# Second MLP of a decoder trunk: a table load that waits for an accumulating transfer

## The chip, the cores and the metric

The kernel runs on one core of a Trainium2 chip. Its time is the device time of one launch in microseconds; the number that is compared is the median over several runs. PE is the matmul engine, DVE and ACT the two elementwise engines, POOL a fourth engine that also writes the descriptors of the transfers that it starts, and SP an engine that does nothing but start transfers. All transfers, whoever starts them, run on the core's 16 DMA engines. An engine works through its own list of instructions in order, and an instruction that waits holds everything behind it on that list.

## The reference

A trunk of two layers over 512 tokens of width 1024, in float32. Layer 0 is attention, layer 1 a gated short convolution, and each is followed by a gated MLP. The change is in the MLP of layer 1:

```python
def conv_ffn(h, norm_g, w_up, conv_w, w_down):
    xn = rms_norm(h, norm_g)
    u = causal_dwconv(xn @ w_up, conv_w)        # w_up: 1024 x 5632, width-3 causal taps
    g, val = u[..., :D_FF], u[..., D_FF:]       # D_FF = 2816
    return (jax.nn.silu(g) * val) @ w_down
```

## The kernel before

**Seven products.** `xn @ w_up` is done as a fast 2x2 block product. The 1024 rows of `w_up` are cut into halves `kh` 0 and 1, and the columns into the gate half and the value half; the tokens are cut into LEFT and RIGHT. Seven products of sums of blocks (called p1, p7, p3, p6, p2, q5 and q4) take the place of eight. The columns are handled in groups of 256 of the gate half and the same 256 of the value half, so the second MLP has 11 groups, g = 0 to 10. Each product is held to float32 accuracy by splitting both sides into a high and a low part in the matmul type and doing three matmuls of the four: 2 column tiles x 4 row tiles x 3 = 24 matmuls of 128x256 for each product, 168 for a group. `halves_to` makes the two parts of a weight tile: ACT writes the high part (`whi_p`, `whi_q`, line 1051), DVE subtracts it from the source for the low part (`wlo_p`, `wlo_q`, line 1053).

**Weight tiles of one group.** Each is 128 x 4 x 256 floats, 512 KB:

- `X` is block (0,0), for p1. Later, POOL's transfer adds block (0,1) to it in place, and it serves q5.
- `Y` comes from a table in DRAM (made earlier in the kernel, from `w_up` alone) and serves p7.
- `three` is a sum of three blocks, from a second table, and serves p6. Later POOL's transfer adds the fourth block (1,0) to it in place; from then on the code calls it `four`, and it serves q4.
- `W` is block (1,0), for p2; `Z` is block (1,1), for p3, whose product is done one group later.

`X`, `Y`, `three`, `W` and `Z` are plain loads, started by SP. The two sums in place ("accumulating transfers", `add_block`, line 1140) are started by POOL. `three`, `W` and `Z` share three buffers: `Z` keeps one, and `three` of group g+1 takes the one that `W` of group g has left, while `W` of g+1 takes the one of `three` of g.

**The schedule.** `slot(g, s)` runs for s = 0 to 6, one product in each slot, in the order p1, p7, p3 (of g-1), p6, p2, q5, q4. The slot also issues the work for products to come. In the order of the code:

- s = 0: SP loads `W` of g, and then `X` and `Y` of g+1.
- s = 1 and 2: the halves of `three` (for p6) and of `W` (for p2); then POOL adds block (1,0) to `three`, which makes it `four`.
- s = 3 and 4: the halves of `X` (for q5) and of `four` (for q4).
- s = 5: `tail` of group g-1 ends with the gated product on DVE (lines 1089 and 1090), and where a block of the down product's operand is complete, POOL starts a transfer that adds one half of the operand to the other, SBUF to SBUF (line 1098, `head_blocks` or `hs_b_blocks`; the "block add" below). Then SP loads `Z` of g, and the halves of `X` of g+1 are made.
- s = 6: `first_sums` makes the halves of `Y` of g+1, POOL adds to `X` of g+1, and SP loads `three` of g+1.

The block adds come in the groups g = 1 to 6 (256 KB each in g = 1, 2, 3 and 5, two of 128 KB in g = 4, one of 128 KB in g = 6). In the second MLP the transfers and the halves' ACT instructions are pinned to the program's order (`pin`), and so the lists of SP and POOL stand as the slots write them. The first MLP uses the same class with `name` 0.

Of the kernel before, what the change touches and what calls it, by code (L numbers as in the profile page):

```python
# [17 lines left out]
F32 = mybir.dt.float32  # L18
# [4 lines left out]
ALU = mybir.AluOpType  # L23
AX = mybir.AxisListType

P = 128
# [9 lines left out]
CHUNK = 1056  # L36
# [21 lines left out]
def trunk(  # L58
# [6 lines left out]
    nc = tc.nc  # L65
# [10 lines left out]
    pin = tc.keep_in_program_order  # L76
    act, dve, pe, pool = InOrder(nc.scalar), InOrder(nc.vector), nc.tensor, nc.gpsimd
# [3 lines left out]
    wp = ctx.enter_context(tc.tile_pool(name="wp", bufs=3))  # L81
# [8 lines left out]
    def bank(tag):  # L90
        n_ps[0] += 1
        return ps.tile([P, S], F32, tag=tag, name=f"ps{tag}{n_ps[0]}", bufs={"a": 2, "b": 4, "c": 2}[tag])
# [125 lines left out]
    def behind(later, earlier):  # L218

        tc.add_manual_dep(  # L220
            later.ins, earlier.ins.name,
            mybir.DependencyInfo(mybir.DependencyClass.NoSync, mybir.DependencyReason.DATA), reason="order",
        )
# [655 lines left out]
    t = bank("c")  # L879
# [4 lines left out]
    t = bank("c")  # L884
# [119 lines left out]
    for g in range(len(units) + 2):  # L1004
# [7 lines left out]
        if g >= 2 and units[g - 2][1] == len(UNITS) - 1:  # L1012
            p = units[g - 2][0]
# [98 lines left out]
    class Sevens:  # L1112
# [20 lines left out]
                pin(made)  # L1133

        def load_one(self, g, n, src):
            t = self.st[g][n] = wp.tile([P, CHUNK], F32, tag="raw", name=f"{n}{self.name}{g}")[:, 0:1024].rearrange("p (k c) -> p k c", c=2 * P)
            self.held(nc.sync.dma_start(t, src))

        def add_block(self, g, n, kh, half):
            tc.keep_in_program_order(nc.gpsimd.dma_start(self.st[g][n], self.block_of(g, kh, half), accum_op=ALU.add))  # L1140
# [61 lines left out]
        def slot(self, g, s):  # L1202

            on, was, soon = (i in self.groups for i in (g, g - 1, g + 1))
            if self.chores:
                self.work_off(self.rate(g, s))
            form, n, fresh = (("p1", "A", True), ("p7", "T", True), ("p3", "R", False), ("p6", "R", False), ("p2", "A", False),
                              ("q5", "R", False), ("q4", "T", False))[s]
            if s == 2:
                if was:  # L1210
                    self.product(g - 1, form, n, fresh)
            elif on:
                self.product(g, form, n, fresh)
            st, p, c = self.st, g - 1, self.st.get(g)
            if s == 0:
                if was:
                    if "p3" not in st[p]:
                        self.weights_of(p, "p3", "Z")
                    self.join(p, "yg", st[p]["T"], st[p]["Xs"])
                    if on and not self.table and g not in self.aside:  # L1220
                        behind(self.joined, self.summed)
                if on:
                    self.load_one(g, "W", self.block_of(g, 1, 0))
                if soon:
                    self.load_pair(g + 1)
            elif s == 1:
                first = not was
                if on and first and not self.ahead and "p6" not in c:
                    self.weights_of(g, "p6", self.sum_of(g))
                if on and not first and self.table:  # L1230
                    self.weights_of(g, "p6", "three")
                if on:
                    act.activation(self.bank_of(g, "R"), c["A"], AF.Copy, scale=-1.0)
                if on and not first and not self.table:
                    self.weights_of(g, "p6", self.sum_of(g))
                if on and first and self.name == 0:
                    self.weights_of(g, "p2", "W")
                if soon and not self.table:
                    self.add_block(g + 1, "Y", 1, 1)
            elif s == 2:  # L1240
                if on:
                    self.kept(g, "P7s", c["T"])
                    if "p2" not in c:
                        self.weights_of(g, "p2", "W")
                    c["four"] = c[self.sum_of(g)]
                    if self.table and soon:
                        self.add_block(g, "four", 1, 0)
                    else:
                        dve.tensor_tensor(c["four"], c["four"], c["W"], op=ALU.add)
            elif s == 3:  # L1250
                if was:
                    self.early(p, st[p]["R"])
                if on:
                    self.weights_of(g, "q5", "X")
                    if not self.table:
                        self.kept(g, "Xs", c["R"])
                        self.weights_of(g, "q4", "four")
                        self.fourth = self.rest
            elif s == 4:
                if on and self.table:  # L1260
                    self.kept(g, "Xs", c["R"])
                    self.weights_of(g, "q4", "four")
            if was and s != 2:
                self.tail(p, s)
            if s == 5:
                if on:
                    self.load_one(g, "Z", self.block_of(g, 1, 1))
                    self.open_wides(g)
                    if soon and not self.table:
                        self.weights_of(g + 1, "p1", "X")  # L1270
                        if g + 1 in self.aside:
                            self.three_of(g + 1)
                    self.left(g, c["A"])
                if soon and self.table:
                    self.weights_of(g + 1, "p1", "X")
                elif on and self.ahead and not soon:
                    self.weights_of(g, "p3", "Z")
            elif s == 6:
                if on:
                    self.join(g, "yv", c["R"], c["P7s"])  # L1280
                if soon:
                    self.first_sums(g + 1)
# [507 lines left out]
    with tc.tile_pool(name="mlp1", bufs=1, reuse_waits="tile") as mp:  # L1790
# [3 lines left out]
        raw = RawForms(up, (place(4, 4), place(8, 4)), s0, s1)  # L1794
# [48 lines left out]
        def slot(g, s):  # L1843
            up.slot(g, s)
            if g == 0 and s in more:
                more[s]()
        mlp(1, norm, mp, (blocks, [(lambda g=g, s=s: slot(g, s)) for g in range(HF + 1) for s in range(7)]))


# [24 lines left out]
```

## Time and profile before

| what | us |
|---|---|
| median of 3 runs (lowest to highest) | 1097.05 (1096.64 to 1101.11) |
| the profiled execution's own time | 1097.78 |
| span of the profiled execution, first to last instruction | 1096.0 |
| PE busy in the span | 1082.0 |
| DVE / ACT / POOL busy in the span | 959.6 / 685.8 / 183.5 |
| second MLP's sum-of-four transfers, first and last start | 765.8 / 948.2 |

The profile lists instructions by engine with their start in us from the span's start. A transfer's row shows the instruction that starts it, on SP ("SPq") or POOL; it lands some us later. In the trace `three` and `four` have one name, `three`: a row of POOL on `three<-in_ffn_w_up` is the accumulating transfer for the sum of four, a row of SP on `three<-t` the table load, and `whi_q<-three` is the first use of the finished sum of four.

### The profile page before, as it was taken

The numbers are of one execution on the slowest core, as the hardware profiler recorded it, in microseconds if no ns is written. First come the engines' busy times: TensorE is split into PE (matmuls) and PEld (weight loads), VectorE is DVE, ScalarE is ACT, GpSimd is POOL, SyncE is SP. The second block draws the span as 40 slices with busy tenths as digits, with TensorE's granted clock in tenths as the row PEclk, the third lists the DMA queues.
The fourth block names the chain that finished last, engine by engine and source line by source line (L and its number), as shares of the span: only waits on it lengthen the run. The fifth ranks groups of instructions, "written<-read, shape, count | busy, mean of one in ns | idle before, by whom it ended". The sixth has DMA issues, their size and how long they took to land.

```text
span 1096.0 us, 21688 instructions
## 1 busy us (share of the span) xinstructions
PE 1082.0 (99%) x8781; PEld 1027.7 (94%) x8781; DVE 959.6 (88%) x1483; ACT 685.8 (63%) x1021; POOL 183.5 (17%) x208
## 2 busy tenths in 40 slices
PE   9999999999999999999999999999999999999998
PEld 7888787879999999999999899999999999999998
DVE  5788898997899888899989889977899899999886
ACT  7466677655466776777557655546656556667653
POOL 4011111111011312014311001001021121014310
PEclk9999999999999999999999999999999999999999
DMA  7668878688767988899974866598879877899961
GB/s 199 163 166 220 188 182 218 163 224 220 202 152 201 223 211 208 214 270 211 232 192 109 181 173 145 137 274 195 218 185 219 184 199 189 219 268 210 239 158 59
DMA packets 178116, 214.21 MB, mean 195 GB/s; under 512 B 7676, under 2 KB 143916, under 8 KB 178016
## 3 DMA queue, kind: packets, MB, share of 16 engines
q0 software_dynamic: 53280, 95.34, 45.4%
q1 hardware_dynamic: 124576, 117.42, 33.8%
q8 instruction: 69, 1.13, 0.4%
q14 instruction: 31, 0.25, 0.1%
q10 hardware_dynamic: 160, 0.07, 0.0%
HBM read 205.72 MB, written 44.04 MB: 228 GB/s over the span
## 4 chain that ended last, share of the span: by engine, by line
PE 71%; DVE 12%; issue 9%; DMA 5%; ACT 2%; POOL 0%; SPq 0%; DVEq 0%; POOLq 0%; ACTq 0%
PE psb L1107 16%; PE psb L357 15%; PE psb L1750 9%; PE psa L1750 8%; PE psa L1107 6%; PE psa L357 4%; DMA three<-in_ffn_w_up 3%; DVE wlo_p L1053 2%; PE psb L733 2%; PE psa L830 2%; DVE wlo L334 1%; PE psc L357 1%; PE psc L805 1%; PE psb L615 1%; DMA Xc<-in_conv_w_in 1%
## 5 line engine op out<-in xcount | busy, mean ns | idle before, releaser
L1107 PE MATMUL psb<-p_hi,wlo_p 128*128 128x256 f32 x480 | 132.5, 276 | 0.9 <-DVE wlo_p L74 0.9
L1107 PE MATMUL psb<-p_hi,whi_p 128*128 128x256 f32 x480 | 132.6, 276 | 0.0
L1107 PE MATMUL psb<-p_lo,whi_p 128*128 128x256 f32 x480 | 132.5, 276 | 0.0
L333 ACT ACTIVATE whi<-raw 128x1024 fp32r<-128x1024 f32 (+2 forms) x77 | 79.0, 1027 | 65.0 <-PE psb L357 22.4
L334 DVE TENSOR_TENSOR wlo<-raw,whi 128x1024 fp32r<-128x1024 f32 (+2 forms) x77 | 90.9, 1180 | 20.2 <-ACT whi L333 20.0
L357 PE MATMUL psb<-hs_a,whi 128*128 128x512 f32 (+1 forms) x312 | 93.3, 369 | 0.0
L1107 PEld LDWEIGHTS psb<-p_hi,wlo_p 128*128 128x128 f32 x480 | 90.0, 188 | 1.2 <-DVE wlo_p L74 1.2
L1107 PE MATMUL psb<-q_hi,wlo_q 128*128 128x256 f32 x320 | 89.4, 279 | 1.1 <-DVE wlo_q L1053 1.1
L1107 PEld LDWEIGHTS psb<-p_hi,whi_p 128*128 128x128 f32 x480 | 90.1, 188 | 0.0
L1107 PEld LDWEIGHTS psb<-p_lo,whi_p 128*128 128x128 f32 x480 | 90.1, 188 | 0.0
L1107 PE MATMUL psb<-q_hi,whi_q 128*128 128x256 f32 x320 | 88.8, 277 | 1.2 <-ACT whi_q L1051 1.0
L1107 PE MATMUL psa<-p_hi,wlo_p 128*128 128x256 f32 x320 | 89.4, 279 | 0.0
L1107 PE MATMUL psa<-p_hi,whi_p 128*128 128x256 f32 x320 | 88.5, 277 | 0.0
L1107 PE MATMUL psb<-q_lo,whi_q 128*128 128x256 f32 x320 | 88.5, 277 | 0.0
L1107 PE MATMUL psa<-p_lo,whi_p 128*128 128x256 f32 x320 | 88.5, 276 | 0.0
L357 PE MATMUL psb<-hs_a,wlo 128*128 128x512 f32 (+1 forms) x208 | 69.5, 359 | 0.0
L1107 PEld LDWEIGHTS psb<-q_hi,wlo_q 128*128 128x128 f32 x320 | 60.0, 188 | 2.3 <-DVE wlo_q L1053 1.8
L357 PEld LDWEIGHTS psb<-hs_a,whi 128*128 128x128 f32 x312 | 52.4, 188 | 10.2 <-issue 3.2
L1750 PE MATMUL psb<-act,whi 128*128 128x256 f32 x352 | 61.1, 278 | 0.7 <-DVE act L1055 0.7
L1107 PEld LDWEIGHTS psb<-q_hi,whi_q 128*128 128x128 f32 x320 | 60.1, 188 | 1.8 <-ACT whi_q L1051 1.2
L1107 PEld LDWEIGHTS psa<-p_hi,wlo_p 128*128 128x128 f32 x320 | 60.0, 188 | 1.0 <-DVE wlo_p L1053 0.6
L1107 PEld LDWEIGHTS psa<-p_hi,whi_p 128*128 128x128 f32 x320 | 60.1, 188 | 0.0
(551 smaller groups left out, 3697.7 us busy)
## 6 DMA issues: line engine op xcount, KB each, us to landing
t<-in_ffn_w_up POOLq DMA_DIRECT2D x24, 768.0 KB, 8.1
raw<-in_attn_w_in SPq DMA_DIRECT2D x24, 512.0 KB, 5.8
t<-in_ffn_w_up POOLq DMA_DIRECT2D x12, 1024.0 KB, 9.8
X<-in_ffn_w_up SPq DMA_DIRECT2D x20, 512.0 KB, 5.1
Y<-t SPq DMA_DIRECT2D x20, 512.0 KB, 6.6
three<-t SPq DMA_DIRECT2D x20, 512.0 KB, 5.9
W<-in_ffn_w_up SPq DMA_DIRECT2D x20, 512.0 KB, 4.0
Z<-in_ffn_w_up SPq DMA_DIRECT2D x20, 512.0 KB, 5.0
```

What stands on the lines that cost most here:

```text
L333: return (act.activation(hi_, raw[:, at_], AF.Copy), dve.tensor_tensor(lo_, raw[:, at_], f32(hi_), op=ALU.subtract))
L334: dve.tensor_tensor(lo_, raw[:, at_], f32(hi_), op=ALU.subtract))
L357: made = [pe.matmul(acc[:, c], w[x], rhs[y][:, c], start=first and x + y + c.start == 0, stop=last and x == 1 and c.stop == S) for x, y in ...
L615: pe.matmul(acc, lhs[0], w[0], start=first, stop=False)
L733: pe.matmul(ss[e][:, c:c + wide], ql[rows, b * P:n], kl[rows, 0:wide], start=first and b == bs[0], stop=last and b == bs[-1])
L805: pe.transpose(t[:, k * P:(k + 1) * P], w[:, e, k * P:(k + 1) * P], ident)
L830: pe.matmul(out_, w, t[:, first:first + step * (NB - k - 1) + 1:step, :], start=k == 0 and i == 0, stop=k == NB - 1 and i == 1)
L1053: rest = dve.tensor_tensor(lo, src, f32(hi), op=ALU.subtract)
L1107: pe.matmul(to, w[a][:, k, c], x[b][:, k, :], start=fresh and i + k + t == 0, stop=i == 1 and k == 3 and t == 2, skip_group_check=not fresh)
L1750: pe.matmul(part, l, r[:, c], start=begin and o + t + c.start == 0, stop=end and t == 2 and o + c.start > 0, skip_group_check=not fresh)
```

## The change

In the slot s = 5 of the second MLP, right after SP's load of `Z` of g, the tile `three` of group g+1 is allocated, and POOL gets a `tensor_tensor` of one column: it writes the first element of each partition of the new `three`, and reads the first element of each partition of `four` of group g. The table load of `three` of g+1 in the slot s = 6 is unchanged but writes over that element, so SP has to wait for the POOL instruction, and the POOL instruction has to wait until the accumulating transfer into `four` of g has landed. What is computed stays the same.

```diff
         def load_one(self, g, n, src):
-            t = self.st[g][n] = wp.tile([P, CHUNK], F32, tag="raw", name=f"{n}{self.name}{g}")[:, 0:1024].rearrange("p (k c) -> p k c", c=2 * P)
-            self.held(nc.sync.dma_start(t, src))
+            if n not in self.st[g]:
+                self.place_one(g, n)
+            self.held(nc.sync.dma_start(self.st[g][n], src))
+
+        def place_one(self, g, n):
+            self.st[g][n] = wp.tile([P, CHUNK], F32, tag="raw", name=f"{n}{self.name}{g}")[:, 0:1024].rearrange("p (k c) -> p k c", c=2 * P)
+
+        def place_three(self, g):
+            self.place_one(g, "three")
+            to, other = self.st[g]["three"][:, 0, 0:1], self.st[g - 1]["four"][:, 0, 0:1]
+            pin(pool.tensor_tensor(to, other, other, op=ALU.add))
...
             if s == 5:
                 if on:
                     self.load_one(g, "Z", self.block_of(g, 1, 1))
+                    if soon and self.name == 1:
+                        self.place_three(g + 1)
                     self.open_wides(g)
```

The lists of PE, DVE, ACT and SP hold the same instructions in the same order as before; POOL's holds ten more. Where they stand on POOL's list, around the sum of four of group 1 (in these names the digit after `three` or `X` is the layer, 1, and the next ones the group; the brackets name the semaphores that an instruction waits on, DMASW those of POOL's transfers, DMAHW those of SP's). Before:

```order
L1140 DMA X11_9542<-in_ffn_w_up 128x4x256 [waits DMAHW0_49,DVE_49,Pool_49]
L1140 DMA three11_9751<-in_ffn_w_up 128x4x256 [waits DMAHW4_49,DMAHW3_49,DMAHW7_49,DMASW5_49,DVE_49]
L1098 DMA head_blocks1_9948<-head_blocks1_9948 128x2x256 [waits DVE_49,PE_49]
L1140 DMA X12_9786<-in_ffn_w_up 128x4x256 [waits DMAHW5_49,DMASW2_49,DVE_49]
L1140 DMA three12_9993<-in_ffn_w_up 128x4x256 [waits DMAHW0_49,DMAHW4_49,DMASW3_49,DVE_49]
```

The same place on POOL's list with the change:

```order
L1149 DMA X11_9542<-in_ffn_w_up 128x4x256 [waits DMAHW0_49,DVE_49,Pool_49]
L1149 DMA three11_9709<-in_ffn_w_up 128x4x256 [waits DMAHW3_49,DMASW5_49,DVE_49]
L1098 DMA head_blocks1_9949<-head_blocks1_9949 128x2x256 [waits DVE_49,PE_49]
L1146 TENSOR_TENSOR three12_9955<-three11_9709 128x1 [waits DMAHW4_49,DMASW5_49,Activation_49]
L1149 DMA X12_9787<-in_ffn_w_up 128x4x256 [waits DMAHW5_49,DMASW2_49,DVE_49]
L1149 DMA three12_9955<-in_ffn_w_up 128x4x256 [waits DMAHW0_49,DVE_49]
```

The new instruction stands behind the sum of four of group 1 and also behind the block add of `head_blocks`, and ahead of the sum into `X` of group 2; the same holds for the new instructions of the groups g = 1 to 6. In the groups without a block add (g = 0, 7, 8 and 9) it stands right behind the sum of four. SP's list at the same place, before:

```order
L1137 DMA Z11_9952<-in_ffn_w_up 128x4x256 [waits DMAHW2_49,DVE_49]
L1137 DMA three12_9993<-t160_1896 128x4x256 [waits DMAHW4_49,DMAHW0_49,DVE_49]
L1137 DMA W12_10026<-in_ffn_w_up 128x4x256 [waits DMAHW1_49,DMASW5_49,DVE_49]
L1128 DMA X13_10028<-in_ffn_w_up 128x4x256 [waits DMASW4_49]
L1129 DMA Y13_10029<-t173_1894 128x4x256 [waits DMAHW3_49]
```

And with the change:

```order
L1138 DMA Z11_9953<-in_ffn_w_up 128x4x256 [waits DMAHW2_49,DVE_49]
L1138 DMA three12_9955<-t160_1896 128x4x256 [waits DMAHW0_49,DMAHW4_49,DVE_49,Pool_49]
L1138 DMA W12_10028<-in_ffn_w_up 128x4x256 [waits DMAHW1_49,DMASW5_49,DVE_49]
L1128 DMA X13_10030<-in_ffn_w_up 128x4x256 [waits DMASW4_49]
L1129 DMA Y13_10031<-t173_1894 128x4x256 [waits DMAHW3_49]
```

The order is the same; the load of `three` has got the wait on POOL, and the loads of `W`, `X` and `Y` stand behind it.

## The prediction

> **What bounds the kernel now.** I read the page first, then the chain of waits inside the second MLP, then POOL's, SP's and ACT's instructions in order of time over one quiet group, and last the DMA engines' work in stretches cut at their pauses. From the page, and from the chain of waits (start us, us, what) at group 4 and at a place where PE runs freely:
>
> ```profile
> PE 1082.0 (99%) x8781; PEld 1027.7 (94%) x8781; DVE 959.6 (88%) x1483; ACT 685.8 (63%) x1021; POOL 183.5 (17%) x208
> ...
> 847.25 1.22 DVE wlo_p L1053
> 849.19 7.63 DMA three<-in_ffn_w_up
> 856.85 1.06 ACT whi_q L1051
> 988.61 2.73 PE psb L1107 x24
> ```
>
> PE is busy almost everywhere, and one product (24 matmuls) takes 2.73 us when nothing is missing, so a group cannot be shorter than 7 x 2.73 = 19.1 us. The chain shows the loop that runs beside it: low part of `three`, sum of four, high part of the sum, and so on. The instant at which the sum of four is first used (I call it L) is seen on ACT (start us, us, what, idle before and what ended it):
>
> ```profile
> 795.34 1.06 ACT L1051 ACTIVATE whi_q<-three 128x1024 fp32r<-128x1024 f32 x1 [0.91 <-DMA three<-in_ffn_w_up]
> 835.29 1.06 ACT L1051 ACTIVATE whi_q<-three 128x1024 fp32r<-128x1024 f32 x1 [1.61 <-DMA three<-in_ffn_w_up]
> 856.85 1.06 ACT L1051 ACTIVATE whi_q<-three 128x1024 fp32r<-128x1024 f32 x1 [3.91 <-DMA three<-in_ffn_w_up]
> 876.48 1.06 ACT L1051 ACTIVATE whi_q<-three 128x1024 fp32r<-128x1024 f32 x1 [1.85 <-DMA three<-in_ffn_w_up]
> 886.68 1.04 ACT L1051 ACTIVATE whi_p<-three 128x1024 fp32r<-128x1024 f32 x1
> 888.63 1.04 ACT L1051 ACTIVATE whi_p<-W 128x1024 fp32r<-128x1024 f32 x1
> 892.09 1.06 ACT L1051 ACTIVATE whi_q<-X 128x1024 fp32r<-128x1024 f32 x1 [0.61 <-DMA X<-in_ffn_w_up]
> 895.96 1.06 ACT L1051 ACTIVATE whi_q<-three 128x1024 fp32r<-128x1024 f32 x1 [1.10 <-DMA three<-in_ffn_w_up]
> 915.49 1.06 ACT L1051 ACTIVATE whi_q<-three 128x1024 fp32r<-128x1024 f32 x1 [1.74 <-DMA three<-in_ffn_w_up]
> ```
>
> ACT waits for the sum of four each time. From L of group 5 to L of group 6 is 895.96 - 876.48 = 19.48 us, 0.4 over the floor of 19.1: PE and this loop are nearly balanced, and a sum that lands later is paid by PE. Group 4 shows it, 856.85 - 835.29 = 21.56. From L of group 1 to L of group 7, the six groups with block adds, it is 915.49 - 795.34 = 120.15, of which 6 x 19.1 = 114.6 are PE's floor. So the most that any change of this loop can save there is 5.5 us.
>
> The DMA engines in stretches of group 5 to 6, and two of group 4 (stretch and its length, then busy time and instructions of PE, PEld, DVE, ACT, POOL, the clock, DMA share, GB/s):
>
> ```profile
> 871.70:872.50 0.80, 0.80 (x10) 0.80 (x9) 0.80 (x2) 0.80 (x2) 0.04 (x1) 1.00 0.11 31
> 872.50:875.90 3.40, 3.40 (x33) 3.40 (x32) 3.00 (x5) 2.13 (x4) 0.00 (x0) 1.00 1.13 180
> 875.90:877.20 1.30, 1.30 (x14) 1.30 (x13) 0.93 (x2) 0.72 (x1) 0.00 (x0) 1.00 0.94 331
> 877.20:879.90 2.70, 2.70 (x24) 2.54 (x24) 2.32 (x3) 2.36 (x3) 0.00 (x0) 1.00 0.01 5
> 879.90:885.20 5.30, 5.30 (x47) 5.17 (x46) 5.26 (x8) 1.06 (x1) 2.50 (x2) 1.00 0.93 270
> 885.20:891.20 6.00, 6.00 (x55) 6.00 (x54) 6.00 (x8) 5.02 (x7) 1.24 (x1) 1.00 1.13 235
> 892.00:895.30 3.30, 3.30 (x32) 3.30 (x31) 2.17 (x4) 2.77 (x4) 0.00 (x0) 1.00 1.12 179
> 851.20:856.50 5.30, 5.30 (x49) 5.30 (x49) 3.87 (x5) 1.74 (x4) 0.00 (x0) 1.00 1.00 197
> 856.50:860.20 3.70, 1.96 (x15) 1.56 (x14) 2.27 (x5) 2.95 (x3) 0.07 (x1) 1.00 0.00 0
> ```
>
> With the issue times below, the rows are read so: 872.5 to 875.9 is the sum of four (3.4 us at 180 GB/s), 875.9 to 877.2 the table load of `three` behind it (1.3 us at 331), then a pause of 2.7, then `W`, `X` and `Y` (5.3 us), then the block add, the sum into `X`, and `Z` (6.0 us). The engines work 3.4 + 1.3 + 5.3 + 6.0 = 16.0 of the 19.4 us between the ends of two sums of four (875.9 and 895.3), and rest 3.4. In group 4 the sum and the table load were mixed (5.3 us for both, not 4.7), and PE then worked 1.96 of 3.70 us, a loss of 1.74.
>
> **The change part by part.** POOL and SP over the same group:
>
> ```profile
> 870.45 1.29 POOL L1140 DMA_DIRECT2D three<-in_ffn_w_up  x1 [6.39 <-DVE wlo_p L1053]
> 880.30 1.19 POOL L1098 DMA_DIRECT2D hs_b_blocks<-hs_b_blocks  x1 [8.56 <-DVE hs_b_blocks L1090]
> 882.04 1.31 POOL L1140 DMA_DIRECT2D X<-in_ffn_w_up  x1 [0.54 <-DVE wlo_p L1053]
> ...
> 871.98 0.37 SPq L1137 DMA_DIRECT2D three<-t  x1
> 878.83 0.37 SPq L1137 DMA_DIRECT2D W<-in_ffn_w_up  x1
> 879.80 0.50 SPq L1129 DMA_DIRECT2D Y<-t  x1
> ```
>
> *Added: ten POOL instructions of one column.* The nearest rows are the kernel's other one-column holds:
>
> ```profile
> L297 POOL TENSOR_TENSOR hold<-raw x2: 927/964/1001, 557.9 to 1052.9; 128x1 f32<-128x1 f32 x2
> L1570 POOL TENSOR_TENSOR hold<-Xc x1: 326/326/326, 707.3 to 707.3; 128x1 f32<-128x1 f32 x1
> ```
>
> So each takes 0.33 to 1.0 us. POOL is 17% busy; what is behind it is the sum into `X`, held at most 0.8 us.
>
> *Moved: the table load of `three`, and with it `W`, `X` and `Y`.* By name the new wait is for the sum of four. But on POOL's list the new instruction stands behind the block add, which waits for DVE's product (8.56 us at 880.30), and that product is made after L. In the groups g = 1 to 6 SP is therefore released when POOL has finished issuing the block add, at 880.30 + 1.19 = 881.49, plus 0.33 to 1.0 for the new instruction: about 882. The load of `three` goes from 871.98 to 882, 10 us later, and `W` from 878.83 to 882.4; `X` and `Y` follow, 3 us later than now. In the groups 0, 7, 8 and 9 SP is released right after L, when the engines rest (2.7 us at 877.2), and a load of 1.3 us fits there.
>
> *What that does to the engines.* They rest from the end of the sum of four, 875.9, to the first bytes of the block add. POOL's issue of the sum of four ends at 870.45 + 1.29 = 871.74 and its bytes begin at 872.5, so 0.76 later; the block add's begin at 881.49 + 0.76 = 882.25. That is a rest of 6.35 us where it was 0.8 and 2.7. From there they have all the work of a group ahead of them, and the next sum of four is the last piece (`Z` and `Y` are issued before it). The new instruction itself is covered: SP's `W` shows first bytes at 879.9, 1.07 after its issue, so the load of `three` is ready at about 883.1, and the block add's 256 KB at 180 GB/s last until 883.7.
>
> With the same work, 16.0 us, the sum of four ends at 882.25 + 16.0 = 898.25, and the loop has 898.25 - 875.9 = 22.35 us where it had 19.4. If `W`, `X` and `Y`, now queued without gaps, each run as `three` did (1.3 us, 3.9 for the 5.3), it is 20.95. `three` ran behind another transfer as these will, so I take a value nearer to the low end, 21.4. PE cannot make it up, for it stands for the sum of four.
>
> *Group by group* (now, then): group 1: its block add was issued until 801.41 by the rows
>
> ```profile
> 800.22 1.19 POOL L1098 DMA_DIRECT2D head_blocks<-head_blocks  x1 [10.13 <-DVE head_blocks L1090]
> 860.12 0.89 POOL L1098 DMA_DIRECT2D head_blocks<-head_blocks  x1 [9.65 <-DVE head_blocks L1090]
> 861.08 0.86 POOL L1098 DMA_DIRECT2D hs_b_blocks<-hs_b_blocks  x1
> 899.25 0.89 POOL L1098 DMA_DIRECT2D hs_b_blocks<-hs_b_blocks  x1 [8.00 <-DVE hs_b_blocks L1090]
> ```
>
> 6.07 after L where group 5 has 881.49 - 876.48 = 5.01, so 21.4 + 1.06, about 22.45. Groups 2, 3 and 5: 21.4 each. Group 4: two block adds until 861.94, 5.09 after L: 21.5. Group 6: until 900.14, 4.18 after L, and half the bytes (0.7 us less): 19.85. Sum 22.45 + 3 x 21.4 + 21.5 + 19.85 = 128.0, against 120.15: **7.85 us lost**; that includes the 1.74 which group 4 gets back, since there the sum of four no longer runs mixed with the table load. The ends are 20.95 (5.15 lost) and 22.35 (13.55 lost). For the groups 7 to 9 I put a gain of 0.4 in all, nearest to group 9's (ACT waited there 2.26, against 1.74 to 1.85 in the quiet groups):
>
> ```profile
> 954.49 1.06 ACT L1051 ACTIVATE whi_q<-three 128x1024 fp32r<-128x1024 f32 x1 [2.26 <-DMA three<-in_ffn_w_up]
> ```
>
> *Is anything else late?* `three` would have its bytes by 883.7 + 1.3 = 885.0 and, with the 0.56 from last byte to use at L (876.46), be there at 885.6; its use is at 886.68. `W` at 886.9, its use 888.63. The sum into `X` would come at about 892, as now (892.09). So the sum of four is the one that is late.
>
> Net: 7.85 - 0.4 = 7.45 on the span: 1096.0 becomes 1103.4. The profiled execution took 1097.78, 1.8 over its span; the median of the runs is 1097.05, so the forecast is 1097.05 + 7.45 = **1104.5 us**, by its own terms 1101.8 to 1110.2.
>
> **The rivals.**
>
> *A: the sums and loads share the engines at a loss.* The block add and the sum into `X` now arrive among four loads. Group 4's row shows 0.6 us more for two mixed transfers; three such pairs in a group would cost up to 1.0 us more in five groups: 1109.5. The Trainium skill, "DMA: Bandwidth & Descriptors", section "Queues, rings and completion order", says that an engine takes turns between its queues packet by packet, which would mix them always. The trace shows both: the mixed stretch at 851.2, and a block add that got nothing until the loads ahead of it were through, since it landed 8.5 us after its issue:
>
> ```profile
> DMA to landing us min/median/max: 8.5/8.5/8.5
> ```
>
> By that rule the sum of four would end no earlier, since all the work is still ahead of it.
>
> *B: the wait is free.* If what is queued were done when the sum of four arrives (about 892), nothing would move: 1097. Against it: from 882.25 to 892 are 9.75 us, and the pieces take at best 6.0 + 4 x 1.3 = 11.2.
>
> *C: the other side, faster.* The table load leaves the engines to the sum of four, which lands sooner: group 4's 1.74 comes back, and the 0.4 us by which each quiet group exceeds PE's floor go in part. That is 1.7 + 6 x 0.2 = 3, about 1094. It decides if SP is released at L and not by the block add. For it speaks that the engines' rest of 2.7 us then takes the load; against it, POOL's list in the six groups.
>
> **How the numbers follow.** Forecast 0.57, A 0.13, B 0.18, C 0.12. Range 1095.5 to 1110.5: it leaves out C and half of A. A measurement of this kernel can tell about 0.5% (5.5 us) from no change, so faster means below 1091.5 and slower above 1102.5. Nearly nine tenths of the forecast and A are slower: 0.50 + 0.13 = 0.63. Faster needs all of the loop's 5.5 us: 0.03. Same is the rest, 0.34.
>
> **What would show it.** SP's load of `three` behind the block add, at about L + 5.5 in the groups 1 to 6 and right after L in 7 to 9; a DMA rest of some 6 us after each sum of four, then no pause until the next one; L to L of 21 to 22 us there, with PE idle before q4. Wrong would be: L to L still at 19.5 with the load that late (the engines were faster than their rows), `three` or `W` awaited by ACT (then p6 or p2 stalls, not q4), or a sum of four that lands while `Y` or `Z` are still under way.

## The result, and the profile after

The changed kernel takes 1111.74 us (median of 4 runs, 1110.49 to 1112.27), the kernel before 1097.24 beside it (1096.64 to 1101.11): a ratio of 1.0118, interval 1.0105 to 1.0131. The medians are 14.5 us apart; the ratio gives 13.0. The direction is the predicted one. The size is nearly twice the forecast's 7.45 us by the medians, 1.7 times by the ratio. The time lies 1.2 us above the range; by the ratio, from the forecast's own 1097.05, it would be 1110.0, just inside it.

The profiled execution took 1110.49 us with a span of 1108.7, 12.7 more than before. ACT's instructions that use the sum of four first (start us, us, what, idle before and what ended it), from group 1 to group 7:

```profile
794.12 1.06 ACT L1051 ACTIVATE whi_q<-three 128x1024 fp32r<-128x1024 f32 x1 [0.56 <-DMA three<-in_ffn_w_up]
817.75 1.06 ACT L1051 ACTIVATE whi_q<-three 128x1024 fp32r<-128x1024 f32 x1 [1.18 <-DMA three<-in_ffn_w_up]
839.46 1.06 ACT L1051 ACTIVATE whi_q<-three 128x1024 fp32r<-128x1024 f32 x1 [2.83 <-DMA three<-in_ffn_w_up]
862.45 1.06 ACT L1051 ACTIVATE whi_q<-three 128x1024 fp32r<-128x1024 f32 x1 [4.04 <-DMA three<-in_ffn_w_up]
884.51 1.06 ACT L1051 ACTIVATE whi_q<-three 128x1024 fp32r<-128x1024 f32 x1 [1.85 <-DMA three<-in_ffn_w_up]
906.65 1.06 ACT L1051 ACTIVATE whi_q<-three 128x1024 fp32r<-128x1024 f32 x1 [2.75 <-DMA three<-in_ffn_w_up]
928.31 1.06 ACT L1051 ACTIVATE whi_q<-three 128x1024 fp32r<-128x1024 f32 x1 [2.37 <-DMA three<-in_ffn_w_up]
```

From L1 to L7 it is 928.31 - 794.12 = 134.2 us where it was 120.15: 14.0 more, the whole loss. L1 itself came 1.2 us earlier than in the kernel before, and what lies behind L7 is 0.1 shorter; both lie outside the change's six groups. The six stretches are 23.6, 21.7, 23.0, 22.1, 22.1 and 21.7. All the loss is where a block add stands ahead of the new instruction, as predicted.

POOL's and then SP's instructions in group 5:

```profile
888.33 1.19 POOL L1098 DMA_DIRECT2D hs_b_blocks<-hs_b_blocks  x1 [10.98 <-DVE hs_b_blocks L1090]
889.06 0.75 POOL L1146 TENSOR_TENSOR three<-three 128x1 f32<-128x1 f32 x1
```

```profile
889.84 0.37 SPq L1138 DMA_DIRECT2D three<-t  x1
890.33 0.92 SPq L1138 DMA_DIRECT2D W<-in_ffn_w_up  x1
891.29 0.68 SPq L1128 DMA_DIRECT2D X<-in_ffn_w_up  x1
892.01 0.57 SPq L1129 DMA_DIRECT2D Y<-t  x1
```

The load of `three` starts 889.84 - 884.51 = 5.33 us after L (predicted: about 5.5), and not because of the sum of four, which landed just ahead of L: the new instruction stands behind the block add, which waited 10.98 us for DVE. `W`, `X` and `Y` follow at once. In group 7, without a block add, the new instruction runs right at L (928.31) and SP behind it:

```profile
928.41 0.19 POOL L1146 TENSOR_TENSOR three<-three 128x1 f32<-128x1 f32 x1 [6.87 <-DVE uv L466]
```

```profile
928.63 0.37 SPq L1138 DMA_DIRECT2D three<-t  x1
```

The DMA engines from group 5 to group 6, cut where their work changes (stretch and its length, busy time and instructions of PE, PEld, DVE, ACT and POOL, the clock, DMA share, GB/s):

```profile
884.20:890.10 5.90, 5.90 (x51) 5.63 (x50) 5.15 (x7) 3.59 (x4) 1.52 (x3) 1.00 0.00 0
890.10:892.20 2.10, 2.10 (x20) 2.10 (x20) 2.10 (x4) 0.54 (x1) 1.26 (x1) 1.00 1.10 155
892.20:895.30 3.10, 3.10 (x30) 3.10 (x29) 3.07 (x5) 1.34 (x2) 0.00 (x0) 1.00 0.98 291
895.30:900.00 4.70, 4.70 (x44) 4.70 (x43) 4.51 (x6) 4.08 (x5) 1.28 (x1) 1.00 1.16 244
900.00:902.60 2.60, 2.60 (x25) 2.60 (x25) 0.82 (x2) 1.46 (x2) 0.00 (x0) 1.00 1.09 373
902.60:905.80 3.20, 2.75 (x24) 2.55 (x24) 3.20 (x5) 1.30 (x3) 0.00 (x0) 1.00 1.12 194
905.80:906.70 0.90, 0.90 (x11) 0.90 (x9) 0.30 (x1) 0.05 (x1) 0.00 (x0) 1.00 0.05 7
```

The engines rest until 890.1, then work without a pause until 905.8: the block add, loads, the sum into `X` mixed with loads, loads, and last the sum of four. Behind it comes only a tail of 0.4 us on about one engine. Cut in the same way, where the work has run out on all but one or two engines, the six stretches are (us):

| group | from L to the first bytes | first bytes to the end of the work | end of the work to next L, with its tail | L to L |
|---|---|---|---|---|
| 1 | 6.7 | 15.6 | 1.35 | 23.6 |
| 2 | 5.65 | 15.6 | 0.45 | 21.7 |
| 3 | 5.65 | 15.6 | 1.75 | 23.0 |
| 4 | 4.75 | 15.9 | 1.4 | 22.1 |
| 5 | 5.6 | 15.7 | 0.85 | 22.1 |
| 6 | 4.75 | 15.9 | 1.0 | 21.7 |
| sum | 33.1 | 94.3 | 6.8 | 134.2 |
| the forecast's own terms | 34.9 | 89.6 | 3.5 | 128.0 |

The work has no pause of more than 0.3 us in it but for group 6, whose 15.9 us contain one of 0.9 (912.2 to 913.1).

### The profile page after: what moved, and what is told of

Same layout as the page of the kernel before. It is cut to its first block, busy times and chain, and to the rows that moved or that the text cites. A ratio compares the mean times of both kernels' runs of the same rounds, so it can differ in the third digit from the quotient of the medians.

```text
span 1108.7 us, 21715 instructions
## 1 busy us (share of the span) xinstructions
PE 1087.7 (98%) x8781; PEld 1031.4 (93%) x8781; DVE 960.3 (87%) x1483; ACT 685.7 (62%) x1021; POOL 187.2 (17%) x218
## 5 line engine op out<-in xcount | busy, mean ns | idle before, releaser
L334 DVE TENSOR_TENSOR wlo<-raw,whi 128x1024 fp32r<-128x1024 f32 (+2 forms) x77 | 90.8, 1179 | 21.5 <-ACT whi L333 21.3
L1107 PEld LDWEIGHTS psb<-q_lo,whi_q 128*128 128x128 f32 x320 | 61.1, 191 | 0.0
```

The source lines that it names most:

```text
L334: dve.tensor_tensor(lo_, raw[:, at_], f32(hi_), op=ALU.subtract))
L1107: pe.matmul(to, w[a][:, k, c], x[b][:, k, :], start=fresh and i + k + t == 0, stop=i == 1 and k == 3 and t == 2, skip_group_check=not fresh)
```

## The experiments

Nine kernels were run; the kernel before ran beside each set, at 1098.6 to 1098.9 us, so ratios are what is compared.

### Ahead of the block add

The block add is held back until the new instruction stands on POOL's list.

```diff
                     if soon and self.name == 1:
                         self.place_three(g + 1)
+                        self.flush()
...
-                blocks.held = not layer and p < HF - 1
+                blocks.held = bool(layer) or p < HF - 1
...
-        up.tail, up.conv = tail, conv
+        up.tail, up.conv, up.flush = tail, conv, blocks.add_up
```

> The change, but in the groups 1 to 6 the new one-column instruction stands ahead of the block add on POOL's list instead of behind it; all else is in the order of the changed kernel. My theory (the cost is the place behind the block add, which holds SP some 5.5 us past the arrival of the sum of four): SP's load of three starts within 1 us of that arrival in all ten groups, W, X and Y start as in the kernel before, the periods from one sum of four to the next are 19.2 to 19.8 us, and the time is 1094 to 1097.5 us. The rival (any delay of the table load behind the sum of four costs it, wherever the instruction stands): 1105 us or more, with periods over 20.5.

Measured: 1097.0 us, ratio 0.9981 (0.9972 to 0.9991). Its POOL and SP in group 4, and ACT's L3, L4 and L7:

```profile
854.26 0.19 POOL L1146 TENSOR_TENSOR three<-three 128x1 f32<-128x1 f32 x1 [4.68 <-DVE uv L466]
857.45 0.90 POOL L1098 DMA_DIRECT2D head_blocks<-head_blocks  x1 [3.00 <-DVE head_blocks L1090]
```

```profile
854.48 0.37 SPq L1138 DMA_DIRECT2D three<-t  x1
```

```profile
834.40 1.06 ACT L1051 ACTIVATE whi_q<-three 128x1024 fp32r<-128x1024 f32 x1 [1.93 <-DMA three<-in_ffn_w_up]
854.15 1.06 ACT L1051 ACTIVATE whi_q<-three 128x1024 fp32r<-128x1024 f32 x1 [2.10 <-DMA three<-in_ffn_w_up]
...
913.05 1.06 ACT L1051 ACTIVATE whi_q<-three 128x1024 fp32r<-128x1024 f32 x1 [1.97 <-DMA three<-in_ffn_w_up]
```

The wait for the sum of four is the same as in the change, ten times, and the loss is gone: SP starts `three` 0.33 us after L. What costs is the place behind the block add. This version also takes 0.2% less than the kernel before. L3 to L4 is 19.75 us (21.56 before), 1.8 less; the stretch L1 to L7, whose L1 is 794.44, is 118.6, 1.5 less. So in this trace the whole gain is the pair of transfers in group 4 that ran mixed before, and the other five groups together gave 0.3 back.

### Without the wait for the sum of four

```diff
-            to, other = self.st[g]["three"][:, 0, 0:1], self.st[g - 1]["four"][:, 0, 0:1]
+            to, other = self.st[g]["three"][:, 0, 0:1], ones
```

> The change, but the new instruction reads a constant instead of the finished sum of four, so that it doesn't wait for that transfer; it stands at the same place, behind the block add in the groups 1 to 6. My theory (the wait for the sum of four never decides in those groups, the list order does): SP's load of three starts as late as in the changed kernel, and the time is its own, 1109 to 1113 us. The rival (the named wait is what costs): back to 1096 to 1099 us.

Measured: 1112.64 us, ratio 1.0124 (1.0107 to 1.0141), the changed kernel's time. Its POOL in group 5:

```profile
889.62 1.19 POOL L1098 DMA_DIRECT2D hs_b_blocks<-hs_b_blocks  x1 [11.13 <-DVE hs_b_blocks L1090]
890.35 0.76 POOL L1146 TENSOR_TENSOR three<-ones 128x1 f32<-128x1 f32 x1
```

The instruction no longer reads the sum of four and runs at the same place, right behind the block add. The wait that the change is named for never decides in these groups.

### Only the groups without a block add

```diff
-                    if soon and self.name == 1:
+                    if soon and self.name == 1 and g in (0, 7, 8, 9):
```

> The new instruction only in the groups 0, 7, 8 and 9, where no block add stands ahead of it; the groups 1 to 6 are as in the kernel before. My theory: the load lands in the rest of the DMA engines there, nothing is lost, 1096.3 to 1097.6 us against 1097.2 of the kernel before. The rival (each held load costs its share of the 14.5 us, 1.45 for each of ten): 1103 us.

Measured: 1098.03 us, ratio 0.9990 (0.9981 to 1.0000). The four new instructions cost nothing. The predicted gain of 0.4 us there is smaller than what this interval can show.

### PE kept busy in group 4

In the changed kernel PE's clock drops once, in group 4. The windows of the changed kernel, clock third from the right:

```profile
862.00:866.00 4.00, 1.69 (x7) 1.48 (x8) 2.46 (x5) 2.95 (x3) 0.27 (x1) 0.75 0.00 0
866.00:870.00 4.00, 4.00 (x21) 4.00 (x20) 4.00 (x6) 0.30 (x1) 3.15 (x4) 0.50 0.65 97
870.00:874.00 4.00, 4.00 (x34) 4.00 (x34) 3.97 (x7) 2.92 (x4) 0.00 (x0) 0.90 1.04 323
```

At the clock of 0.50 only 21 matmuls start in 4 us, where group 5's row above has 44 in 4.7. It looked like a second cost of the late sum, so it was taken away:

```diff
+                if s == 6 and self.name == 1 and g == 4:
+                    spare = bank("c")
+                    for _ in range(18):
+                        pe.matmul(spare[:, 0:HT], self.st[g]["q5"][0][:, 0, 0:P], self.forms["q5"][0][:, 0, :], start=True, stop=True)
```

> The change, with 18 matmuls of q5's shape that nothing reads (18 x 0.113 = 2.0 us, work that isn't part of the computation) between q5 and q4 of group 4, where PE stood idle for 2.1 us and the granted clock then was 0.50 for some 7 us. The theory that the low clock is paid for: the clock stays at 1.0 there, and the time falls by 2.5 to 3 us against the changed kernel, to about 1108.9. The theory that the loop of transfers sets the time and the low clock lies beside it: the clock stays at 1.0 and the time is within 0.5 us of the changed kernel's, 1111.2 to 1112.2.

Measured: 1113.71 us, ratio 1.0138 (1.0122 to 1.0153), no faster than the changed kernel. The same windows here, and ACT's L4 and L5:

```profile
862.00:866.00 4.00, 3.69 (x31) 3.29 (x29) 1.00 (x2) 1.84 (x2) 0.00 (x0) 1.00 0.09 12
866.00:870.00 4.00, 3.46 (x27) 3.30 (x28) 4.00 (x8) 1.77 (x3) 2.10 (x3) 1.00 0.26 37
```

```profile
864.16 1.06 ACT L1051 ACTIVATE whi_q<-three 128x1024 fp32r<-128x1024 f32 x1 [4.10 <-DMA three<-in_ffn_w_up]
885.91 1.06 ACT L1051 ACTIVATE whi_q<-three 128x1024 fp32r<-128x1024 f32 x1 [1.85 <-DMA three<-in_ffn_w_up]
```

The clock stayed at 1.00, and L4 to L5 is 21.75 us against 22.06: 0.3, not 2.5 to 3. The low clock lies beside the loop of transfers, which sets when the next sum of four comes. (The matmuls of the two kernels' ends stand in a slightly different order, so the whole times are a rougher guide here than the stretch.)

### Two groups alone

```diff
-                    if soon and self.name == 1:
+                    if soon and self.name == 1 and g in (2, 5):
```

> The new instruction, behind the block add as in the changed kernel, only in the slots of the groups 2 and 5; the other groups are as in the kernel before. If each late load costs its own group's stretch and nothing else: two of the six losses, 2.3 to 2.6 us each, so about 1102 us against 1097.2 of the kernel before, with the loss in the periods L2 to L3 and L5 to L6 alone. If the losses of neighbouring groups feed each other (a late load of one group pushing the next one's): clearly less, 2 us or under, about 1099.

Measured: 1106.83 us, ratio 1.0066 (1.0052 to 1.0081): 7.9 us by the medians, 7.3 by the ratio, for two of the six groups. The loss is where it was expected, L2 to L3 and L5 to L6, but these are 24.75 and 23.6 us, 5.4 and 4.1 more than before instead of 2.3 to 2.6. ACT's L2 and L3, then POOL's and SP's start of the two transfers ahead of L3:

```profile
815.74 1.07 ACT L1051 ACTIVATE whi_q<-three 128x1024 fp32r<-128x1024 f32 x1 [1.00 <-DMA three<-in_ffn_w_up]
840.49 1.06 ACT L1051 ACTIVATE whi_q<-three 128x1024 fp32r<-128x1024 f32 x1 [6.00 <-DMA three<-in_ffn_w_up]
```

```profile
829.23 1.29 POOL L1149 DMA_DIRECT2D three<-in_ffn_w_up  x1 [6.63 <-DVE wlo_p L1053]
```

```profile
830.75 0.37 SPq L1138 DMA_DIRECT2D three<-t  x1
```

A held load alone is dearer, since the next one is not held: it is queued at 830.75 while the late work is still being done, and its bytes share the engines with the sum of four. From L2 the work now ends 22.8 us later (838.5) instead of the changed kernel's 21.3, and from there to L3 it takes 2.0 instead of 0.45. So neither expectation was right. In the changed kernel, as I read it, each hold also keeps the next table load away from the sum of four and so pays back part of the loss; no run takes that one load away.

### A small block add

The block add keeps 32 of its 256 columns; the rest of that sum is left out.

```diff
         def add_up(self):
+            w = 32 if self.layer else HT
             for k0, k1 in self.sums:
                 tc.keep_in_program_order(
-                    nc.gpsimd.dma_start(self.block("b", k0, k1 - k0), self.block("a", k0, k1 - k0), accum_op=ALU.add))
+                    nc.gpsimd.dma_start(self.block("b", k0, k1 - k0)[:, :, 0:w], self.block("a", k0, k1 - k0)[:, :, 0:w], accum_op=ALU.add))
```

> The change, with block adds of 32 columns instead of 256 in the second MLP (the rest of that sum is left out of the computation). POOL's list is the same, so SP is released as late as in the changed kernel; the DMA engines have 224 KB less to do in five groups and 112 KB less in group 6, which at the 180 GB/s of an accumulating transfer is 1.25 and 0.6 us. If the amount of work behind the rest sets the end of the sum of four, the stretch from L1 to L7 (134.2 us in the changed kernel) falls by 5 x 1.25 + 0.6 = 6.9 us, and the time to about 1105. If the chain of single latencies (release, first bytes, landing) sets it, or the block add runs beside the others for nothing: within 1 us of the changed kernel, 1111 to 1113.

Measured: 1108.26 us, ratio 1.0083 (1.0066 to 1.0100). ACT's L1 and L7:

```profile
794.68 1.06 ACT L1051 ACTIVATE whi_q<-three 128x1024 fp32r<-128x1024 f32 x1 [0.51 <-DMA three<-in_ffn_w_up]
...
925.63 1.06 ACT L1051 ACTIVATE whi_q<-three 128x1024 fp32r<-128x1024 f32 x1 [2.20 <-DMA three<-in_ffn_w_up]
```

The stretch L1 to L7 is 130.95 us, 3.2 less than in the changed kernel: half of the 6.9 that the amount of work would give, and more than nothing. An estimate from the traces gives a likely reason: in the changed kernel's group 5 the load of `three` is queued at 889.84, and where its bytes found the engines free they came 1.0 us after that (912.10 to 913.1 in group 6), so it could have begun at about 890.85. The block add's bytes run from 890.1 to 891.9. So some 0.75 of its 1.8 us fill time in which the engines have nothing else, and only the rest can be saved.

### Only W, X and Y late

```diff
             self.place_one(g, "three")
-            to, other = self.st[g]["three"][:, 0, 0:1], self.st[g - 1]["four"][:, 0, 0:1]
-            pin(pool.tensor_tensor(to, other, other, op=ALU.add))
+            self.place_one(g, "W")
+            pin(pool.tensor_tensor(self.st[g]["W"][:, 0, 0:1], ones, ones, op=ALU.add))
```

> The new instruction stands behind the block add as in the changed kernel, but writes into the tile of W, not into that of three: the table load of three starts as in the kernel before, and only W, and X and Y behind it on SP's list, wait for the block add (3 us later than in the kernel before instead of 10). My theory: the load of three is worked off in the DMA engines' rest again, so 1.3 us less lie ahead of the next sum of four, or up to 1.8 with what a mixed load takes; the periods of the six groups are 20.7 to 21.2, and the time is 1104 to 1107 us. The rival (only the load of three is what must not be late): 1097 to 1099 us. The other rival (W, X and Y being late is all that counts): 1111 to 1113.

Measured: 1104.35 us, ratio 1.0045 (1.0031 to 1.0060), about 5.4 us lost by the medians, 4.9 by the ratio. SP in group 3, and ACT's L1 and L7:

```profile
841.88 0.37 SPq L1138 DMA_DIRECT2D three<-t  x1
844.87 0.37 SPq L1138 DMA_DIRECT2D W<-in_ffn_w_up  x1
```

```profile
796.83 1.06 ACT L1051 ACTIVATE whi_q<-three 128x1024 fp32r<-128x1024 f32 x1 [0.48 <-DMA three<-in_ffn_w_up]
...
922.52 1.06 ACT L1051 ACTIVATE whi_q<-three 128x1024 fp32r<-128x1024 f32 x1 [1.47 <-DMA three<-in_ffn_w_up]
```

The stretch is 125.7 us, 20.95 a group in the mean (20.15 to 22.56), as my theory had it. The lateness of `W`, `X` and `Y` alone costs 125.7 - 120.15 = 5.5 us; with that of `three` on top, which then isn't loaded in the engines' rest any more, it is 134.2, another 8.5. The loss grows with the work that is pushed out of the rest.

### The loads ahead of the block add

The version with the new instruction ahead of the block add, but in the groups 1 to 6 the new instruction reads one column of DVE's finished product (`newest`) instead of the sum of four.

```diff
+            if 1 <= g - 1 <= 6:
+                other = self.newest(2 * (g - 2) + 1)
```

> In the groups 1 to 6 the new instruction waits for DVE's product (it reads the product's tile) and stands right ahead of the block add, so SP is released 0.6 to 0.9 us earlier than in the changed kernel, and the block add starts 0.6 to 0.75 us later; all else is as in the changed kernel. In the changed kernel's trace the DMA engines run the block add alone for 1.8 us before the loads' first bytes come, and group 6, with half a block add, has 0.9 us of it and then a pause. If the start of the loads sets the end of the sum of four: each of the six stretches is 0.6 to 0.9 us shorter, L1 to L7 falls from 134.2 to 129 to 131, and the time to about 1108 us. If the block add's start sets it, as my prediction counted: 0.6 to 0.75 us longer each, about 1116. If only the amount of work counts: within 1 us of 1112.

Measured: 1110.49 us, ratio 1.0101 (1.0084 to 1.0118). The profiled execution was the longest of its four (1115.14); its L1 and L7 are 134.3 us apart, as in the changed kernel. ACT's L3 and L4, and the engines between them (the first load bytes come at 849.7):

```profile
844.79 1.06 ACT L1051 ACTIVATE whi_q<-three 128x1024 fp32r<-128x1024 f32 x1 [2.87 <-DMA three<-in_ffn_w_up]
867.07 1.06 ACT L1051 ACTIVATE whi_q<-three 128x1024 fp32r<-128x1024 f32 x1 [1.62 <-DMA three<-in_ffn_w_up]
```

```profile
849.70:854.20 4.50, 4.50 (x41) 4.39 (x40) 4.46 (x7) 1.52 (x2) 1.75 (x2) 1.00 0.93 250
854.20:861.20 7.00, 7.00 (x64) 7.00 (x63) 6.15 (x8) 4.83 (x7) 1.28 (x1) 1.00 1.15 246
861.20:865.80 4.60, 2.85 (x25) 2.65 (x24) 2.02 (x3) 2.76 (x4) 0.00 (x0) 1.00 1.09 239
```

The loads' first bytes come 4.9 us after L, against 7.6 in the changed kernel's group 3, where the block add's come at 5.65. But the block add's bytes are then done among the others, and the work takes 16.1 us, not 15.6. The theory that the block add's start sets the end (1116) falls. Between the other two the run doesn't decide. The ratio of 1.0101 lies at what 1108 us would be (1.0098) and under the changed kernel's 1.0118, though the intervals overlap; the stretch of 134.3 us, seen in the one execution with a profile, is that of the amount of work and not the 129 to 131 of the loads' start. In this trace the first five groups together are 1.6 us longer than in the changed kernel, and group 6 is 1.5 us shorter (932.61 - 912.43 = 20.2): there the loads come before the half block add, the pause of 0.9 us is gone, and the work takes 14.6 us.

### One group ahead

The version with the new instruction ahead of the block add, but with that instruction in group 4 alone.

```diff
                     if soon and self.name == 1:
-                        self.place_three(g + 1)
+                        if g == 4:
+                            self.place_three(g + 1)
+                        self.flush()
...
```

> The new instruction ahead of the block add, in the slot of group 4 alone, where the table load and the sum of four ran mixed in the kernel before (L3 to L4 was 21.56 us); all other groups as in the kernel before. If the gain of the version with the instruction ahead of every block add is this one pair of transfers: the stretch L3 to L4 falls to 19.7 us, and the time is 1.8 us under the kernel before, a little better than that version, ratio 0.9984. If the other groups gain too: less than half of that, ratio 0.9992 or more.

Measured: 1097.54 us, ratio 0.9987 (0.9977 to 0.9998), and L3 to L4 is 20.2 us in its trace (854.58 - 834.38), 1.36 less than before. That is most of the gain of the version with all groups (0.9981), with one instruction; the two intervals overlap, so a gain in other groups is neither shown nor excluded.

## Why the prediction was right in direction and wrong in size

**Right: where and how.** SP's release behind the block add, 5.3 us after L in group 5; the rest of the engines; no pause from then to the next sum of four but the one in group 6; stretches of about 22 us; nothing lost in the groups 7 to 9. PE waits ahead of q4 in four of the six stretches, most in group 4 (wait of PE for the high part of the sum of four: us in total, times, longest):

```profile
PE psb L1107 <- ACT whi_q L1051: 2.1, 1, 2.1
```

Before L2 it was p2 that stood, see below, and before L5 PE ran at half clock. The two runs that move the instruction ahead of the block add and that take its named wait away show that the place on POOL's list is the cause, they don't only agree with it.

**Wrong: the work behind the rest.** The step that failed is "`three` ran behind another transfer as these will, so I take a value nearer to the low end, 21.4". It put 15.05 us of work behind the rest; the traces show 15.6 to 15.9, just under the "same work" of 16.0 that stood beside it as the upper end. Over six groups that is 94.3 against 89.6, 4.7 of the 6.2 us that were missing. Queued loads do run faster, but only the later ones: 373 GB/s in 900.0 to 902.6, and 291 in 892.2 to 895.3. At 524 kB a load these are 1.4 and 1.8 us, not 1.3. And in group 6 the "half the bytes (0.7 us less)" saved nothing: its work took 15.9, because the loads start 1.8 us behind the block add's first bytes (913.1 and 911.35) and the half block add fills only part of that. The run with the small block add shows the same from the other side.

**Wrong: the landing.** The forecast took 0.56 us from last byte to use, from one quiet group. After the change it is 0.45 to 1.75 with the tail, 6.8 in all against 3.5. In group 3 the tail looks so:

```profile
860.70:862.10 1.40, 0.76 (x7) 0.56 (x5) 0.00 (x0) 0.00 (x0) 0.00 (x0) 1.00 0.08 12
```

A share of 0.08 is about one of the 16 engines at work for 1.4 us, while ACT waits. The Trainium skill, "DMA: Bandwidth & Descriptors", section "Why a DMA increments its semaphore by 16 and not by 1", says that the engines finish independently and that only the last of 16 reports makes the transfer complete; the row agrees. In the quiet groups of the kernel before, the next load's bytes follow the sum of four at once, so whether it had such a tail can't be seen there; why the last engine is late was not tested.

**The start** was 1.8 us better than its term (33.1 against 34.9), mostly in group 4, whose first block add had its bytes 1.1 us sooner. It hid that much of the other two misses.

**"Nothing else is late"** was wrong. `W` was awaited in one group, `three` in another, and the sum into `X` in five:

```profile
810.73 1.06 ACT L1051 ACTIVATE whi_p<-W 128x1024 fp32r<-128x1024 f32 x1 [3.09 <-DMA W<-in_ffn_w_up]
...
879.89 1.06 ACT L1051 ACTIVATE whi_q<-X 128x1024 fp32r<-128x1024 f32 x1 [1.53 <-DMA X<-in_ffn_w_up]
...
895.58 1.06 ACT L1051 ACTIVATE whi_p<-three 128x1024 fp32r<-128x1024 f32 x1 [0.78 <-DMA three<-t]
```

The first made PE wait 0.76 us in p2, which the prediction had named as a sign of being wrong. No run takes these waits away alone. What speaks against a cost of their own is that the DMA engines go on working through them: in the groups 1 to 5 no pause of more than 0.3 us lies between the block add and the sum of four.

**The rivals.** A's 1109.5 is the nearest number, but its mechanism is not seen where it was looked for: in 895.3 to 900.0 the sum into `X` and loads ran mixed at 244 GB/s, 1147 kB in 4.7 us; apart they would take 524 kB at 180 GB/s and 623 at 331, together 4.8. B fell at once. C's mechanism is real but needs another order on POOL: the version with the instruction ahead of the block add has the gain of group 4 (1.8 us, predicted 1.7), not the 0.2 in each of the other groups.

## What to carry to other kernels

A wait holds back what is behind it on its list, and it is itself behind what stands ahead of it: look at the waiting engine's list before pricing the wait's name, since here the named transfer decided nothing and the place behind the block add cost 14 us. When work is pushed out of a resource's pause into a loop that is nearly balanced, price it by the full amount of work, and let a faster rate count only for the pieces whose rate a trace has shown in that place. And a single held transfer may be dearer than a row of them (5.4 and 4.1 us here, where the same two groups lost 2.3 and 2.7 in the row): the next load, not held, then shares the engines with the sum that everything waits for.

## What was not expected of the hardware

- The granted clock fell to 0.50 at 864.0, in group 4. PE had run out of work 2.5 us earlier, had waited 2.10 us and just started two matmuls again. At 870.8 the clock was back. The Trainium skill, "TensorE: Matmul & The Clock Gate", Part 1, states half rate after at least one idle window of about 3.4 us; here the pause was shorter, and 3.4 us before the fall PE was still at work. And some 7 us of half clock cost nothing that could be measured, as the run with PE kept busy shows.
- A transfer's last bytes can trail by 1.4 us at 12 GB/s on about one engine's share, and what waits for it waits for that tail.
- The first loads behind the block add ran at 291 GB/s, the last ones ahead of the sum of four at 373. Why was not tested.
